# Delta-rule layer: the squares of a head's output placed behind the Xd copy of the next head's solve

## The chip, the cores and the metric

The kernel runs on one core of one Trainium2 chip. The metric is the device time of one execution in microseconds. A core has five engines that work side by side, each through its own queue in order: TensorE (PE; its weight loads are shown apart as PEld), VectorE (DVE), ScalarE (ACT), GpSimd (POOL) and SyncE (SP, which issues most transfers). An engine that waits for a semaphore holds back all that stands behind it in its queue.

## The reference, cut to what matters

The program is a trunk of two layers, each a token mixer and a squared-ReLU MLP, on 512 tokens of 1024 channels. The change lies in the first mixer, a bidirectional gated delta rule with 8 heads of 128 channels:

```python
def _rmsnorm(x, g):
    return x * lax.rsqrt(jnp.mean(x * x, axis=-1, keepdims=True) + RMS_EPS) * g.astype(F32)

def _mixer_gdn(h, w_in, conv_w, a_log, dt_bias, norm_g, w_out):
    ...
    o_f = _gated_delta_chunked(q, k, v, beta[0], g[0])
    o_b = _flip(_gated_delta_chunked(_flip(q), _flip(k), _flip(v), _flip(beta[1]), _flip(g[1])))
    o = (o_f + o_b).transpose(0, 2, 1, 3)
    o = _rmsnorm(o, norm_g) * jax.nn.silu(z.reshape(bn, s, A_HEADS, A_DV))
    return jnp.matmul(o.reshape(bn, s, A_VW).astype(w_out.dtype), w_out)
```

Inside `_gated_delta_chunked` each chunk solves a unit lower triangular system, and a recurrence over the chunks gives the output. The squares of the change are those of `_rmsnorm`: per head, the sums over 128 channels of `o * o` for each of the 512 tokens.

## The kernel before

Products with weights run on PE as three passes: each fp32 operand is split into a high part (a cast on ACT, L96) and a low part (a subtraction on DVE, L101), and `mm3` (L122 to L124) issues high x high, high x low and low x high. These are the *streaming* matmuls of the delta-rule stage: 128x512, 24 for each of the projections to k, q, v and z of a head (tiles pjk, pjq, pjv, pjz), and the output projection (oa).

Each head has four parts. `project` computes k, q, v, z with their short convolutions (DVE, L1405), a Silu on ACT (L1443, with a table load before it and another, L55, behind it) and, in `rows`, the transposes of k and q (tile ktp, L1463), their copy (kt, L1466), their squares (L1468, sums to ssp) and some small exponentials (neg, kds, fq). `solve` inverts the triangular matrices of both directions: it starts from 4x4 blocks, transposes them (xp, L1572), copies them (Xd, L1574), and then doubles the block size in levels of 4, 8, 16, 32 and 64. A level has one product of ath and Dd and two products of Xd and pz (all tile lv, L1600, of 8 matmuls of 128x64 each); a masked copy of the first product to pz stands between (on DVE, but ACT does it at 32, L1614, and a half at 64, L1630). After level 64, ACT copies to Dd (L1635), and a correction product follows (tile nw, L1646). `recur` runs the recurrence (tiles m, vd, vn, sn) and ends with the output product op (L1730), which stays in one PSUM bank of a pool of two. `finish` squares the four 128x128 pieces of op on ACT with an accumulated sum (L1742: junk is thrown away, oss is kept), forms the inverse root (rsy, L196 and L197, and small DVE operations), scales op with it (fo, L1748), transposes (otp, L1752) and multiplies with Silu of z and the norm's weight.

The loop of `gdn` interleaves heads: in round i it issues `recur` of head i-2, `solve` of head i-1, `project` of head i and `finish` of head i-2, in this order; the pairs that the parts yield are not used by `run`. This order of the text is not that of the engines. The framework's scheduler lays out each engine's queue from the dependencies, the order of the text and its own costs, and so a moved instruction moves others. Heads are counted from 0; "in head h" below means within the solve of head h, where the output of head h-1 is squared.

The steps that are touched are ahead of everything in `finish`, and, in `solve`, the copy to Xd:

```python
            T.transpose(xp[:, u, :], dd[:, u, :], g.idh)
        xd = t8("Xd", 1)
        A.copy(xd, xp)
```

Of the kernel before, what the change touches and what calls it, by code (L numbers as in the profile page):

```python
# [8 lines left out]
F32 = mybir.dt.float32  # L9
# [3 lines left out]
AF = mybir.ActivationFunctionType  # L13
# [4 lines left out]
P = 128  # L18
# [3 lines left out]
NT = S // P  # L22
# [1305 lines left out]
def gdn(c, w_in, conv_w, a_log, dt_bias, norm_g, w_out, ln_g, ln_b, x, w_next):  # L1328
    tc, nc = c.tc, c.nc
    with c.banks(ch=2, pj=3, tp=1, ac=2), tc.tile_pool(name="gdn", bufs=1) as pool:  # L1330
        g = GdnConst(c, pool, w_in, a_log, dt_bias, conv_w, norm_g, x)
        hi = [c.big.tile([P, 2, S], F32R, name=f"oh{t}", tag=f"xt{t}") for t in range(NT)]
        lo = [pool.tile([P, 2, S], F32R, name="ol", tag="ol", bufs=NT) for t in range(NT)]
        heads = [GdnHead(c, pool, g, h, w_in, hi[h // 2][:, h % 2, :], lo[h // 2][:, h % 2, :]) for h in range(A_H)]
        for a, b in zip(heads, heads[1:] + [GdnHead(c, pool, g, A_H, w_in, None, None)]):
            a.next = b
        lhs = lambda k, sl: (hi[k // 2][:, k % 2, sl], lo[k // 2][:, k % 2, sl])
        z = [[None, None] for t in range(NT)]
        early = list(range(6))

        def load_z(hf):
            if hf:
                tl = pool.tile([P, NT, S], F32, name="z", tag="sil", bufs=3)
            else:
                tl = heads[-1].next.kq
                more = [heads[-1].t2(tag, n).rearrange("p n i -> p (n i)") for tag, n in (("kt", 3), ("qd", 4))]
            for t in range(NT):
                z[t][hf] = tl[:, t, :] if hf or t < 2 else more[t - 2]
                c.dma(z[t][hf], x[t * P:(t + 1) * P, 512 * hf:512 * hf + 512])

        def run(*gens):
            for gen in gens:
                for _ in gen:
                    pass

        done = set()
        for i in range(A_H + 2):
            old, mid, new = (heads[j] if 0 <= j < A_H else None for j in (i - 2, i - 1, i))
            if old:
                run(old.recur(done))  # L1360
            if mid:
                run(mid.solve(done))
            if new:
                run(new.project(done))
            if i >= A_H:
                load_z(i - A_H)
                run(c.out_pieces(w_out, early, lhs, z, "pj", (i - A_H,), 1))
            if old:
                run(old.finish(done))
        par = c.load_ln(ln_g, ln_b, lambda j: pool.tile([P, S], F32, name="lnp", tag=("ath", "atl", "a4", "Xd")[j]))  # L1370
        c.new_x()
        c.new_xt()
        c.out_last(w_out, [[6, 7]] * 2, lhs, z, ("pj", "ac"), par,
                   [(pool, "oah", "oal", 1), (pool, "ol", "ol", NT)], ahead=lambda: c.take_ahead(w_next, 3))


class GdnHead:
# [8 lines left out]
    def t8(self, name, bufs):  # L1386
        return self.pool.tile([P, 2 * NT, P], F16, name=name, tag=name, bufs=bufs)
# [121 lines left out]
    def solve(self, done):  # L1509

        c, pool, g, h = self.c, self.pool, self.g, self.h
        V, A, T = c.nc.vector, c.nc.scalar, c.nc.tensor
# [59 lines left out]
            T.transpose(xp[:, u, :], dd[:, u, :], g.idh)  # L1572
        xd = t8("Xd", 1)
        A.copy(xd, xp)  # L1574

        def half(t, s, i):

# [95 lines left out]
    def recur(self, done):  # L1673


        c, pool, g, h = self.c, self.pool, self.g, self.h
        V, A, T = c.nc.vector, c.nc.scalar, c.nc.tensor
        ps = self.bank("ktp", tag="tp")
        for n in range(NT):
            T.transpose(ps[:, n, :], self.v[:, n * P:(n + 1) * P], c.ident)  # L1680
        self.vt = self.t2("vt", 2)
        A.copy(self.vt, ps)
        yield 0.0, 1.0
        states, vns = [{}, {}], [{}, {}]
        cur = [None, None]
        for step in range(NT):
            ns = (step, NT - 1 - step)
            rhs = [self.vt[:, n, :] for n in ns]

            def both(name, ops):  # L1690

                ps = self.bank(name, shape=(P, 2, P), tag="ch")
                for d in range(2):
                    T.matmul(ps[:, d, :], *ops(d), start=True, stop=True)  # L1694
                return ps

            if step:
                m1 = both("m1", lambda d: (self.kc(ns[d]), cur[d]))
                for d, n in enumerate(ns):
                    rhs[d] = pool.tile([P, P], F32, name="r", tag="r", bufs=3)  # L1700
                    V.scalar_tensor_tensor(rhs[d], m1[:, d, :], self.pos[:, n, d:d + 1], self.vt[:, n, :], ALU.mult, ALU.subtract)
                yield 0.45, 0.6
            vds = [None, None]
            m2 = both("m2", lambda d: (self.xf[:, d * NT + ns[d], :], rhs[d]))
            for d, n in enumerate(ns):
                states[d][n] = cur[d]
                if step < NT - 1:
                    vds[d] = pool.tile([P, P], F32, name="vd", tag="vd", bufs=3)
                    A.mul(vds[d], m2[:, d, :], self.kds[:, n, d:d + 1])
            for d, n in enumerate(ns):  # L1710
                vn = pool.tile([P, P], F32, name="vn", tag="vn", bufs=9)
                A.mul(vn, m2[:, d, :], -1.0 if step else 1.0)
                vns[d][n] = vn
            yield 0.45, 1.0
            if step < NT - 1:
                m3 = both("m3", lambda d: (self.kt[:, ns[d], :], vds[d]))
                for d, n in enumerate(ns):
                    sn = pool.tile([P, P], F32, name="sn", tag="sn", bufs=10)
                    if cur[d] is None:
                        A.copy(sn, m3[:, d, :])  # L1720
                    else:
                        V.scalar_tensor_tensor(sn, cur[d], g.egl[:, n, d, h:h + 1], m3[:, d, :], ALU.mult, ALU.subtract)
                    cur[d] = sn
                yield 0.45, 0.6
        self.op = op = self.bank("op", tag="ch")
        for n in (1, 2, 0, 3):
            mm = [(self.qke[d][:, n, :], vns[d][n]) for d in range(2)]
            mm += [(self.qd[d][:, n, :], states[d][n]) for d in range(2) if states[d][n] is not None]
            for i, (l, r) in enumerate(mm):
                T.matmul(op[:, n, :], l, r, start=i == 0, stop=i == len(mm) - 1)  # L1730
            if n == 2:
                yield 1.8, 0.0
        done.add(("op", h))

    def finish(self, done):

        c, pool, g, op = self.c, self.pool, self.g, self.op
        V, A, T = c.nc.vector, c.nc.scalar, c.nc.tensor
        ss = c.small.tile([P, NT], F32, name="oss", tag="ss")
        junk = pool.tile([P, P], F32, name="junk", tag="junk", bufs=2)  # L1740
        for n in range(NT):
            A.activation(junk, op[:, n, :], AF.Square, accum_out=ss[:, n:n + 1])  # L1742
        rs_ = c.small.tile([P, NT], F32, name="ors", tag="rs")
        V.tensor_tensor(ss, ss, self.fq2, ALU.mult)
        c.rsqrt(rs_, ss, NT, RMS_EPS, self.fq)
        on = self.t2("fo", 1)
        for n in range(NT):
            A.mul(on[:, n, :], op[:, n, :], rs_[:, n:n + 1])  # L1748
        yield 1.6, 6.0
        otp = self.bank("otp", tag="ch")  # L1750
        for n in range(NT):
            T.transpose(otp[:, n, :], on[:, n, :], c.ident)  # L1752
        p = pool.tile([P, S], F32, name="p", tag="on", bufs=2)
        otp = otp.rearrange("p n i -> p (n i)")
        n = 1 if self.h < A_H - 1 else 2
        for i in range(n):
            sl = slice(i * S // n, (i + 1) * S // n)
            V.scalar_tensor_tensor(p[:, sl], otp[:, sl], g.ng[:, 0:1], self.sz[:, sl], ALU.mult, ALU.mult)
            A.copy(self.ohi[:, sl], p[:, sl])
        for i in range(n):  # L1760
            sl = slice(i * S // n, (i + 1) * S // n)
            V.tensor_tensor(self.olo[:, sl], p[:, sl], self.ohi[:, sl].bitcast(F32), ALU.subtract)
        done.add(("finish", self.h))
        yield 0.45, 0.0
# [39 lines left out]
```

## Time and profile before

| | |
|---|---|
| median of 3 runs | 1340.54 us (1340.32 to 1341.0) |
| the profiled execution, its own time | 1341.23 us |
| its span in the profile | 1339.4 us |
| granted TensorE clock | 0.996 |
| PE busy, first 105 us | 99.79 us |
| PE busy, 400 us to the end (939.40 us) | 924.64 us |
| DMA share, 105 to 400 us / 400 us to the end | 0.20 / 0.53 |

The delta-rule layer takes the first 410 us; the rows between 105 and 400 us, quoted in the prediction, are the rounds in which squares of a head's output stand. How to read the rows: a timeline row has the start in us, the duration in us, the engine, line, operation, tiles as out<-in with their shapes, and the count of merged instructions; in brackets stands the idle time before and what ended it. A row of a table by windows has the stretch, its span, and the busy time and count for PE, PEld, DVE, ACT and POOL, then the granted clock, the DMA share and GB/s. A row of groups has the busy time and mean ns, then the idle time before it and its releasers. An activation with an accumulated sum appears as two records, the ACTIVATE and the reading of its accumulator.

### The profile page before, as it was taken

How to read it: one execution, taken by the hardware profiler on the slowest of the kernel's cores; microseconds unless marked ns; L12 is line 12 of the kernel's file. 1: busy time of each engine (PE TensorE's matmuls, PEld its weight loads, DVE VectorE, ACT ScalarE, POOL GpSimd, SP SyncE). 2: the span in 40 equal slices, each digit the busy share in tenths (PEclk: the TensorE clock that was granted, in tenths of full speed). 3: DMA queues.
4: the chain of work that ended last, by engine and by line, in shares of the span. 5: the costliest groups of instructions: out<-in, count | busy, mean ns of one | idle time of the engine just before them, and what ended most of it. 6: DMA issues, size and time to landing. Idle time of an engine off the chain costs nothing.

```text
span 1339.4 us, 22232 instructions
## 1 busy us (share of the span) xinstructions
PE 1317.2 (98%) x8629; PEld 1124.4 (84%) x8629; DVE 1099.9 (82%) x1802; ACT 800.5 (60%) x1590; POOL 123.3 (9%) x177
## 2 busy tenths in 40 slices
PE   8999999999999999999999999999999999999996
PEld 8777878777777889999998888888889899999985
DVE  6797878788778878988988877967879678989888
ACT  4667657767643645666566754654456456565656
POOL 4000000000000910100102100000001001101011
PEclk9999999999999999999999999999999999999998
DMA  6221112112232674775748532221327475757556
GB/s 179 64 65 47 35 46 64 48 49 72 72 96 63 210 161 149 161 179 150 171 124 176 138 111 71 63 64 63 94 64 208 107 186 137 165 170 147 156 136 148
DMA packets 155660, 154.35 MB, mean 115 GB/s; under 512 B 7723, under 2 KB 122531, under 8 KB 155555
## 3 DMA queue, kind: packets, MB, share of 16 engines
q1 hardware_dynamic: 143779, 110.85, 27.8%
q0 software_dynamic: 11776, 42.08, 16.1%
q8 instruction: 68, 1.11, 0.3%
q14 instruction: 37, 0.30, 0.1%
HBM read 113.99 MB, written 2.10 MB: 87 GB/s over the span
## 4 chain that ended last, share of the span: by engine, by line
PE 86%; DVE 6%; ACT 6%; issue 1%; DMA 1%; DVEq 0%; POOL 0%; ACTq 0%; POOLq 0%
PE pX L123 3%; PE pX L122 3%; PE pX L124 3%; PE fx L124 3%; PE fx L123 3%; PE fx L122 3%; PE pjv L123 3%; PE m L1694 3%; PE pjv L122 3%; PE pjv L124 3%; PE pj L123 3%; PE pj L124 3%; PE pj L122 3%; PE fyz L124 2%; PE fyz L122 2%; PE fyz L123 2%
## 5 line engine op out<-in xcount | busy, mean ns | idle before, releaser
L101 DVE TENSOR_TENSOR wl<-wst,wh 128x1024 fp32r<-128x1024 f32 x148 | 182.3, 1232 | 49.1 <-ACT wh L96 47.8
L96 ACT CAST wh<-wst 128x1024 fp32r<-128x1024 f32 x150 | 157.7, 1051 | 101.1 <-PE fyz L123 30.1
L101 DVE TENSOR_TENSOR w2l<-w2r,w2h 128x1024 fp32r<-128x1024 f32 x92 | 112.7, 1225 | 27.2 <-ACT w2h L96 27.1
L96 ACT CAST w2h<-w2r 128x1024 fp32r<-128x1024 f32 x94 | 98.4, 1048 | 56.3 <-PE pX L124 24.8
L402 POOL DMA_DIRECT2D w2r<-w2r x56 | 48.4, 891 | 503.1 <-DVE w2l L101 290.1
L96 ACT CAST ah<-h 128x1024 fp32r<-128x1024 f32 x56 | 58.8, 1051 | 51.8 <-PE pZ L123 23.2
L451 DVE TENSOR_TENSOR wst<-wst 128x512 f32<-128x512 f32 x110 | 73.5, 688 | 0.2
L101 DVE TENSOR_TENSOR al<-h,ah 128x1024 fp32r<-128x1024 f32 x56 | 68.6, 1224 | 5.2 <-ACT ah L96 5.2
L123 PE MATMUL pX<-w2l,ah 128*128 128x512 f32 x168 | 66.1, 394 | 0.0
L122 PE MATMUL pX<-w2h,ah 128*128 128x512 f32 x168 | 66.0, 393 | 0.0
L124 PE MATMUL pX<-w2h,al 128*128 128x512 f32 x168 | 65.7, 391 | 0.0
L123 PE MATMUL pj<-xtl,wh 128*128 128x256 f32 (+1 forms) x192 | 64.6, 338 | 0.6 <-DVE xtl L188 0.6
L122 PE MATMUL pj<-xth,wh 128*128 128x256 f32 (+1 forms) x192 | 64.2, 338 | 0.3 <-ACT xth L187 0.2
L124 PE MATMUL pj<-xth,wl 128*128 128x256 f32 (+1 forms) x192 | 64.5, 337 | 0.0
L122 PE MATMUL pjv<-wh,xth 128*128 128x512 f32 x128 | 54.4, 425 | 0.0
L124 PE MATMUL pjv<-wh,xtl 128*128 128x512 f32 x128 | 50.2, 392 | 0.0
L123 PE MATMUL pjv<-wl,xth 128*128 128x512 f32 x128 | 50.0, 390 | 0.0
L124 PE MATMUL fx<-xh,wl 128*128 128x256 f32 x176 | 49.7, 283 | 0.0
L124 PE MATMUL fyz<-xh,wl 128*128 128x256 f32 x176 | 49.7, 282 | 0.0
L124 PE MATMUL fx<-xth,wl 128*128 128x256 f32 x176 | 49.7, 282 | 0.0
L123 PE MATMUL fx<-xtl,wh 128*128 128x256 f32 x176 | 49.7, 282 | 0.0
L122 PE MATMUL fyz<-xh,wh 128*128 128x256 f32 x176 | 49.7, 282 | 0.0
(528 smaller groups left out, 4319.1 us busy)
## 6 DMA issues: line engine op xcount, KB each, us to landing
wst<-in_mlp_w SPq DMA_DIRECT2D x68, 512.0 KB, 4.9
w2r<-in_mlp_w SPq DMA_DIRECT2D x60, 512.0 KB, 4.4
w2r<-w2r POOLq DMA_DIRECT2D x56, 512.0 KB, 5.6
wst<-in_a_w_in SPq DMA_DIRECT2D x32, 512.0 KB, 4.0
wst<-in_b_w_in SPq DMA_DIRECT2D x32, 256.0 KB, 3.0
wst<-in_a_w_out SPq DMA_DIRECT2D x8, 512.0 KB, 3.6
wst<-in_b_w_in SPq DMA_DIRECT2D x8, 512.0 KB, 4.2
wst<-in_b_w_out SPq DMA_DIRECT2D x8, 512.0 KB, 3.7
```

Source lines behind the costliest of these rows:

```text
L96: h = nc.scalar.copy(hi, src)
L101: self.halves = h, nc.vector.tensor_tensor(lo, src, hi.bitcast(F32), ALU.subtract)
L122: mm(ps, ah, bh, start=start, stop=False, **kw)
L123: mm(ps, ah, bl, start=False, stop=False, **kw)
L124: self.last_mm = mm(ps, al, bh, start=False, stop=stop, **kw)
L402: nc.gpsimd.dma_start(blocks[a + (q,)], blocks[b + (q,)], accum_op=ALU.add)
L451: plus = lambda a, b: V.tensor_tensor(a, a, b, ALU.add)
L1694: T.matmul(ps[:, d, :], *ops(d), start=True, stop=True)
```

## The change

`finish` loses its squares; a new method `squares` has them, with a tile tag of their own for the sums. `solve` calls it for the head before right behind its Xd copy, so that in the order of the text the squares of head h-1 come ahead of the rest of the solve of head h and of `project` of head h+1. The last head has no solve after it, and its squares stay in `finish`.

```diff
         for a, b in zip(heads, heads[1:] + [GdnHead(c, pool, g, A_H, w_in, None, None)]):
-            a.next = b
+            a.next, b.prev = b, a
+        heads[0].prev = None
...
         xd = t8("Xd", 1)
         A.copy(xd, xp)
+        if self.prev:
+            self.prev.squares()
...
+        self.oss = None
         done.add(("op", h))
+
+    def squares(self):
+
+        c, op = self.c, self.op
+        self.oss = ss = c.small.tile([P, NT], F32, name="oss", tag="oss")
+        junk = self.pool.tile([P, P], F32, name="junk", tag="junk", bufs=2)
+        for n in range(NT):
+            c.nc.scalar.activation(junk, op[:, n, :], AF.Square, accum_out=ss[:, n:n + 1])
 
     def finish(self, done):
 
         c, pool, g, op = self.c, self.pool, self.g, self.op
         V, A, T = c.nc.vector, c.nc.scalar, c.nc.tensor
-        ss = c.small.tile([P, NT], F32, name="oss", tag="ss")
-        junk = pool.tile([P, P], F32, name="junk", tag="junk", bufs=2)
-        for n in range(NT):
-            A.activation(junk, op[:, n, :], AF.Square, accum_out=ss[:, n:n + 1])
+        if self.oss is None:
+            self.squares()
+        ss = self.oss
```

The instructions of every engine are the same in kind and number; their order is not. In the changed kernel a line has a number that is higher by 1 (from the loop in `gdn` on), by 3 (from behind the Xd copy) or by 11 (in `finish`). ACT in head 3, from the Xd copy on, before:

```order
L1574 COPY Xd<-xp 128x1024
L96 CAST wh<-wst 128x1024
L1401 ACTIVATE sil<-pjq,cw 128x512
L96 CAST wh<-wst 128x1024
L1614 CAST pz_135<-lv 32x4x32 x4
L1443 ACT_TABLE_LOAD
L1443 ACTIVATE sil<-sil 128x2048
L1630 ACTIVATE pz_137<-lv 64x4x64
L55 ACT_TABLE_LOAD
L1635 CAST Dd<-lv 64x4x64 x2
```

and now:

```order
L1745 ACTIVATE junk,oss<-op 128x128 x2
L1575 COPY Xd<-xp 128x1024
L1745 ACTIVATE junk,oss<-op 128x128 x2
L96 CAST wh<-wst 128x1024
L1402 ACTIVATE sil<-pjq,cw 128x512
L196 ACTIVATE rsy<-oss,bias_77 128x4
L197 ACTIVATE rsy<-rsy 128x4
L1617 CAST pz_135<-lv 32x4x32 x4
L1633 ACTIVATE pz_137<-lv 64x4x64
L1444 ACT_TABLE_LOAD
L1444 ACTIVATE sil<-sil 128x2048
L1638 CAST Dd<-lv 64x4x64 x2
```

Two squares stand ahead of the Xd copy and two behind it; the first table load and the Silu have moved behind the last pz copy, the other table load behind the Dd copies, and one cast of a weight is gone from here.

ACT in head 5, from the pz copies of level 32 to the Dd copies, before:

```order
L1614 CAST pz_135<-lv 32x4x32 x4
L1468 ACTIVATE junk,ssp<-ktp 128x128
L1742 ACTIVATE junk,oss<-op 128x128
L1468 ACTIVATE junk,ssp<-ktp 128x128
L1742 ACTIVATE junk,oss<-op 128x128
L1468 ACTIVATE junk,ssp<-ktp 128x128
L1742 ACTIVATE junk,oss<-op 128x128
L96 CAST wh<-wst 128x1024
L1630 ACTIVATE pz_137<-lv 64x4x64
```

and now:

```order
L1617 CAST pz_135<-lv 32x4x32 x4
L96 CAST wh<-wst 128x1024
L1402 ACTIVATE sil<-pjv,cw 128x512
L1444 ACT_TABLE_LOAD
L1444 ACTIVATE sil<-sil 128x2048
L1633 ACTIVATE pz_137<-lv 64x4x64
L55 ACT_TABLE_LOAD
L1467 COPY kt<-ktp 128x512
L1638 CAST Dd<-lv 64x4x64 x2
```

The squares are gone, those of k and q come after the Dd copies, and the Silu with its two table loads and the copy of the transposed k stand here instead.

PE in head 5, from the last level product to the correction product nw, before:

```order
L1600 MATMUL lv<-Xd,pz_137 128x64
L122 MATMUL pjz<-xth,wh 128x512
L123 MATMUL pjz<-xtl,wh 128x512
L1646 LDWEIGHTS ath
L1646 MATMUL nw<-Dd,ath 128x128
```

and now:

```order
L1603 MATMUL lv<-Xd,pz_137 128x64
L124 MATMUL pjz<-xth,wl 128x512
L122 MATMUL pjz<-xth,wh 128x512
L123 MATMUL pjz<-xtl,wh 128x512
L124 MATMUL pjz<-xth,wl 128x512
L1649 LDWEIGHTS ath
L1649 MATMUL nw<-Dd,ath 128x128
```

Four streaming matmuls stand between the two products instead of two. The order of PE differs from the solve of head 1 on and is the same again behind the last head's transposes (otp).

## The prediction

> **What bounds the kernel now.** I read the page's busy shares and its chain first, then a table of the delta-rule stage alone, then the timelines of TensorE (PE) and ScalarE (ACT) around the places that the new order changes.
>
> ```profile
> span 1339.4 us, 22232 instructions
> PE 1317.2 (98%) x8629; PEld 1124.4 (84%) x8629; DVE 1099.9 (82%) x1802; ACT 800.5 (60%) x1590; POOL 123.3 (9%) x177
> PE 86%; DVE 6%; ACT 6%; issue 1%; DMA 1%; DVEq 0%; POOL 0%; ACTq 0%; POOLq 0%
> 105.00:400.00 295.00, 292.74 (x2571) 232.89 (x2571) 236.19 (x501) 191.16 (x554) 2.37 (x4) 1.00 0.20 58
> L1742 ACT ACTIVATE junk<-op 128x128 f32<-128x128 f32 x28 | 8.1, 289 | 2.8 <-PE op L1730 2.7
> ```
>
> PE sets the end: busy 98% of the span, 86% of the chain. The fourth row is the stage with the squares (from 105 to 400 us: span, then PE, PEld, DVE, ACT and POOL busy, granted clock 1.00): PE 292.74 of 295.00. ACT works 191.16 of these 295 us, so it has room on average; the 28 squares that the last row counts cost it 8.1 us there and are not what the time is made of. The change leaves the work of every engine as it is. It can only move the short waits of PE, and the page's idle understates them, since a matmul's end is modelled. They are read from start to start:
>
> ```profile
> 120.05 0.50 PE L123 MATMUL pjk<-xtl,wh 128*128 128x512 f32 x1
> 120.68 0.22 PE L1646 MATMUL nw<-Dd,ath 128*128 128x128 f16 x1
> ...
> 293.34 0.48 PE L122 MATMUL pjz<-xth,wh 128*128 128x512 f32 x1
> 293.65 0.40 PE L123 MATMUL pjz<-xtl,wh 128*128 128x512 f32 x1
> 294.41 0.22 PE L1646 MATMUL nw<-Dd,ath 128*128 128x128 f16 x1 [0.36 <-ACT Dd L1635]
> ...
> 380.49 0.40 PE L122 MATMUL oa<-wh,oh 128*128 128x512 f32 x1
> 380.95 0.22 PE L1646 MATMUL nw<-Dd,ath 128*128 128x128 f16 x1
> ...
> 199.24 0.39 PE L123 MATMUL pjz<-xtl,wh 128*128 128x512 f32 x1
> 199.62 0.28 PE L1600 MATMUL lv<-pz,Xd 128*128 128x64 f16 x4
> 200.17 0.28 PE L1600 MATMUL lv<-pz,Xd 128*128 128x64 f16 x4 [0.27 <-ACT pz L1614]
> ...
> 331.38 0.39 PE L124 MATMUL pjz<-xth,wl 128*128 128x512 f32 x1
> 331.99 0.33 PE L1463 MATMUL ktp<-ident,sil 128*128 128x128 f32 x1 [0.22 <-ACT junk L1468]
> ```
>
> A streaming 128x512 matmul lets the next one start 0.23 us later (0.31 when it is the first after short ones: 293.34 to 293.65). Before the correction product nw the step is 0.63 us in head 1, 0.76 in head 5 and 0.46 in head 7: PE waits for ACT's Dd copies. Over heads 1 to 7 (the first and the last of the seven are quoted) the steps exceed 0.23 by 2.2 us, and those of heads 2 to 6, by the same reading, by 1.55. Waits of the same kind stand before the level products (200.17) and the transposes of k (331.99).
>
> **The change part by part.** *What moves.* Four squares per head leave their places between the squares of k and q and go behind (or, where the output is there early, in front of) the Xd copy of the next solve. The order shows that for heads 0 to 5; the squares of head 6 keep their places, one ahead of Xd and three behind, and those of head 7 stay in `finish`. No DMA moves past another but one weight load ahead of two loads of x at the very end of the stage, which I cost at nothing: these loads have the whole output projection before their first use. No table load is added: the count of ACT instructions is the same. I go through the places where the new order makes PE wait or spares a wait.
>
> *Xd held by two squares (heads 2, 3 and 5).* The xp transposes run right behind the output product, and Xd now queues behind two squares.
>
> ```profile
> 188.39 0.39 PE L1730 MATMUL op<-sn,qd 128*128 128x128 f32 x2
> 189.06 0.40 PE L1600 MATMUL lv<-Dd,ath 128*128 128x64 f16 x8
> 189.30 0.48 PE L122 MATMUL pjq<-xth,wh 128*128 128x512 f32 x1
> 190.33 0.41 PE L1600 MATMUL lv<-pz,Xd 128*128 128x64 f16 x8
> ...
> 189.26 1.01 ACT L1574 COPY Xd<-xp 128x1024 f16<-128x1024 f16 x1 [3.13 <-PE xp L1572]
> ...
> 364.92 0.39 PE L1730 MATMUL op<-sn,qd 128*128 128x128 f32 x2
> 365.34 0.28 ACT L1742 ACTIVATE junk<-op 128x128 f32<-128x128 f32 x1 [2.68 <-PE op L1730]
> 365.62 1.01 ACT L1574 COPY Xd<-xp 128x1024 f16<-128x1024 f16 x1
> 366.53 0.28 ACT L1742 ACTIVATE junk<-op 128x128 f32<-128x128 f32 x1
> 366.94 0.28 ACT L1742 ACTIVATE junk<-op 128x128 f32<-128x128 f32 x1
> ```
>
> Head 7 has the new pattern already, with one square: it starts 0.42 after the last pair of op starts (364.92 to 365.34), Xd 0.28 behind it; two squares stand 0.41 apart. In head 3 that gives 188.39 + 0.42 + 0.41 + 0.28 = 189.50 for Xd, against 189.26. There the product with Xd starts 190.33, just as Xd ends (190.27), four streaming matmuls behind the product before it, so the 0.24 reaches PE; head 5 has the same cover, head 2 seven matmuls, which hide it. **+0.48 us**, bounded by 0 (the squares end with xp) and 1.4 (0.69 in both).
>
> *Squares of k and q alone.*
>
> ```profile
> 330.77 0.30 ACT L1742 ACTIVATE junk<-op 128x128 f32<-128x128 f32 x1
> 331.02 0.30 ACT L1468 ACTIVATE junk<-ktp 128x128 f32<-128x128 f32 x1
> 331.27 0.32 ACT L1742 ACTIVATE junk<-op 128x128 f32<-128x128 f32 x1
> ...
> 335.17 0.28 ACT L1468 ACTIVATE junk<-ktp 128x128 f32<-128x128 f32 x1
> 335.57 0.28 ACT L1468 ACTIVATE junk<-ktp 128x128 f32<-128x128 f32 x1
> ```
>
> Alternating squares start 0.25 us apart, squares into one accumulator 0.40. Taking one of a pair away thus saves 0.10, not 0.25. In head 2 three stand alone before the last pz copy, which makes it 0.3 later, and three small exponentials now come ahead of the Dd copies, some 0.2 more: **+0.5** (0 to 0.75).
>
> *Table loads between the last pz copy and the Dd copies.* With the squares gone the scheduler finds other gaps for the loads around Silu.
>
> ```profile
> 203.38 0.38 ACT L1630 ACTIVATE pz<-lv 64x256 f16<-64x256 f32 x1
> 203.77 1.28 ACT L55 ACT_TABLE_LOAD   x1
> 205.07 0.76 ACT L1635 CAST Dd<-lv 64x256 f16<-64x256 f32 x2
> 205.73 0.58 ACT L1466 COPY kt<-ktp 128x512 f32<-128x512 f32 x1
> ...
> 201.43 1.92 ACT L1443 ACTIVATE sil<-sil 128x2048 f32<-128x2048 f32 x1
> ...
> 341.57 1.06 ACT L1443 ACTIVATE sil<-sil 128x1024 f32<-128x1024 f32 x1
> ```
>
> The Dd copies need the last two level products; a product takes PE 0.24 (189.06 to 189.30). Head 5: load 1.28, kt 0.48 (0.58 less the 0.10 that it overlaps its neighbour, 205.07 + 0.76 to 205.73) and Dd 0.76 make 2.52 us behind pz; PE has the two products (0.48) and four streaming matmuls (0.31 + 3 x 0.23) there, 1.48, so nw waits about **1.0**. Head 3: load, Silu and Dd make 3.96; PE has three streaming matmuls, the products, eleven streaming ones and two short ones, 4.1, of which 0.45 have passed when pz ends: **0.3**. Head 6, with the short Silu (1.06) and three small exponentials (0.4), has 3.5 against 5 + 8 streaming matmuls and the products, 3.6, of which 0.7 have passed: **0.6**. Sum +1.9; 0 if Dd's own input is the later, 3.0 if the loads also wait for their input.
>
> [...]
>
> *More changes of stream.* Counted in the order, streaming and short matmuls change over 521 times in the stage instead of 517; at 0.08 (0.31 less 0.23): **+0.3**.
>
> *Gains.* In front of nw heads 2 to 6 now have 3, 11, 3, 4 and 8 streaming matmuls instead of 2, 3, 2, 2 and 4. Each hides 0.23, so the 1.55 us of waits there go (what replaces them is charged above): **-1.55** (0 to -2.2). Of the waits at the level products, head 3's cast of a weight ahead of the pz copies is gone, head 4 has seven matmuls of cover instead of three, and in head 6 the k transposes stand elsewhere: I take -0.35, -0.5 and -0.5, with -0.2 for head 5: **-1.55** (0 to -3).
>
> *Sum.* 0.48 + 0.5 + 1.9 + 0.3 - 1.55 - 1.55 = +0.1 us. The profiled execution took 1341.23 us (span 1339.4), 0.69 over the median 1340.54 of the three runs, so the forecast on the median is **1340.6 us**.
>
> **The rivals.** *Faster by the covers.* The scheduler lengthened the covers where PE waited; if the input of Dd is later than ACT in heads 3, 5 and 6, the 1.9 and the 0.5 fall away: 1340.54 + 0.8 - 3.1 = 1338.2, and with all bounds of the gains 1336.1; I write 1337. For it: the longer covers at five of seven places. Against: the loads stand in ACT's order ahead of Dd, and ACT runs in order. Chance 0.16.
>
> *Slower through ACT's chain.* One mechanism: behind Xd, ACT's way to the Dd copies gets longer in every solve, because the squares stand alone (0.15 more for each of four squares of k and q, 0.6 a head) and the table loads have come in between. It decides from the point where the step before nw exceeds the 0.76 of today's worst. Six heads at about 0.45 beyond my 3.2, with the gain at nw alone: 3.2 + 2.7 - 1.55 = +4.4, 1344.9 us. For it: ACT already releases most of PE's waits here. Against: PE's order gives it more matmuls to wait with. Chance 0.15. [...]
>
> **How the numbers follow.** A measurement of this kernel tells about 0.2%, 2.7 us, from no change. The forecast, gains and losses that cancel within that, has 0.66; faster 0.16, slower 0.15 and 0.02, and 0.01 for what I have not seen. With every term at its lower bound the sum is -4.9, with every term at its upper +5.5; half way from the forecast that is 1338.1 to 1343.3, and I reach 0.6 further on both sides, into the two rivals: range 1337.4 to 1343.8. Faster 0.15, same 0.67, slower 0.18.
>
> **What would show it.** Xd in heads 3 and 5 starts about 1.1 us behind the last pair of op, and the product with Xd about 0.24 later than now. The step before nw is 0.23 to 0.31 in heads 2 and 4, over 0.5 in heads 3, 5 and 6. PE's busy time between 105 and 400 us stays within 1 us. [...]

## The result and the profile after

| | before | changed |
|---|---|---|
| median of 20 runs each | 1340.1 us | 1342.55 us |
| ratio, 95% interval | | 1.0018 [1.0012, 1.0025] |
| the profiled execution, its own time | 1341.23 us | 1342.4 us |
| its span, granted clock | 1339.4 us, 0.996 | 1340.7 us, 0.997 |

The changed kernel takes 2.45 us more than the kernel before. That is inside the range and below the 0.2% that the prediction set as the bound, and yet the interval lies wholly above 1: a small loss, which 20 runs of each can tell from none. One of the 20 runs of the changed kernel took 1608.05 us at a granted clock of 0.849, and the ratio leaves it out. The page of the changed kernel (span; busy time, share and count by engine; the chain by engine):

```profile
span 1340.7 us, 22227 instructions
PE 1317.6 (98%) x8629; PEld 1122.6 (84%) x8629; DVE 1100.4 (82%) x1802; ACT 801.9 (60%) x1590; POOL 123.3 (9%) x177
PE 86%; DVE 6%; ACT 5%; DMA 1%; issue 1%; SPq 0%; DVEq 0%; ACTq 0%
```

Its table by windows (stretch, its length, busy time and count of PE, PEld, DVE, ACT and POOL, granted clock, DMA share, GB/s):

```profile
105.00:400.00 295.00, 292.88 (x2563) 232.47 (x2562) 236.71 (x502) 192.52 (x554) 2.37 (x4) 1.00 0.20 58
```

In the stage that the change reorders PE's busy time is 292.88 us, 0.14 more than before. Such a window cuts both kernels at the same clock time, not at the same work. I therefore cut at PE's instructions. Four of them stand in the same place of PE's order in both kernels: the first transpose of xp in head 1, the last otp of the delta-rule layer, the first projection pj of the first MLP, and the last matmul of the program. First before, then the changed kernel, each from PE's timeline:

```profile
104.96 0.51 PE L1572 MATMUL xp<-idh,Dd 128*128 128x128 f16 x6
...
410.04 0.27 PE L1752 MATMUL otp<-ident,fo 128*128 128x128 f32 x1
...
425.39 0.40 PE L122 MATMUL pj<-xth,wh 128*128 128x256 f32 x2
...
1327.71 0.39 PE L124 MATMUL pX<-xh,al 128*128 128x512 f32 x1
```

```profile
103.98 0.51 PE L1573 MATMUL xp<-idh,Dd 128*128 128x128 f16 x6
...
409.15 0.27 PE L1763 MATMUL otp<-ident,fo 128*128 128x128 f32 x1
...
424.49 0.40 PE L122 MATMUL pj<-xth,wh 128*128 128x256 f32 x2
...
1328.96 0.39 PE L124 MATMUL pX<-xh,al 128*128 128x512 f32 x1
```

From xp to otp, the stage that holds every reordered instruction: 305.08 us before, 305.17 now. From otp to pj: 15.35 and 15.34. From pj to the last matmul: 902.32 before, **904.47** now. (These two executions also differ by 0.98 us ahead of xp; that moves from execution to execution: pj starts at 425.39 and 424.49 here, at 423.22 and 423.40 in the next two kernels.) The loss lies behind the stage, where PE runs the same instructions in the same order. No single step between two matmuls there has grown by more than 0.013 us. The 2.15 us are spread over 5251 steps, 0.4 ns each on average, and no wait stands out. The tile view (durations min/median/max in ns, then first and last start) shows it on one product of the MLPs, before and then changed:

```profile
L122 PE MATMUL fyz<-xh,wh x176: 277/282/388, 505.2 to 1282.6; 128*128 128x256 f32 x176
```

```profile
L122 PE MATMUL fyz<-xh,wh x176: 279/284/387, 504.5 to 1283.7; 128*128 128x256 f32 x176
```

The median is 2 ns longer, the minimum too.

What reaches that far is the one part of the diff that the prediction did not cost: the name of the tile for the sums. The sums had shared the name "ss"; now they have a name of their own, with four buffers of 32 bytes in each partition. In the built programs all tiles of the layers' pools therefore lie 128 bytes higher (h of the first MLP at byte 95104 instead of 94976 of a partition), while the split weights (wh, wl) and the split input of the projections (xth, xtl), which lie ahead of them, stay where they were.

### The profile page after: what moved, and what is told of

It reads as the page before. It is cut to its first block, busy times and chain, and to the rows that moved or that the text cites. A ratio compares the mean times of both kernels' runs of the same rounds, so it can differ in the third digit from the quotient of the medians.

```text
span 1340.7 us, 22227 instructions
## 1 busy us (share of the span) xinstructions
PE 1317.6 (98%) x8629; PEld 1122.6 (84%) x8629; DVE 1100.4 (82%) x1802; ACT 801.9 (60%) x1590; POOL 123.3 (9%) x177
## 4 chain that ended last, share of the span: by engine, by line
PE 86%; DVE 6%; ACT 5%; DMA 1%; issue 1%; SPq 0%; DVEq 0%; ACTq 0%
PE pX L122 3%; PE pX L124 3%; PE pX L123 3%; PE fx L124 3%; PE fx L123 3%; PE fx L122 3%; PE pjv L123 3%; PE pjv L122 3%; PE pjv L124 3%; PE m L1697 3%; PE pj L123 3%; PE pj L124 3%; PE pj L122 3%; PE fyz L122 2%; PE fyz L123 2%; PE fyz L124 2%
## 5 line engine op out<-in xcount | busy, mean ns | idle before, releaser
L123 PE MATMUL fx<-xl,wh 128*128 128x256 f32 x176 | 49.8, 283 | 0.0
L123 PE MATMUL fyz<-xl,wh 128*128 128x256 f32 x176 | 49.7, 283 | 0.0
L122 PE MATMUL fx<-xh,wh 128*128 128x256 f32 x176 | 49.7, 282 | 0.0
```

The source lines that it names most:

```text
L122: mm(ps, ah, bh, start=start, stop=False, **kw)
L123: mm(ps, ah, bl, start=False, stop=False, **kw)
```

## The experiments

### Place against order

The first three kernels separate the two: the kernel before with the new name only, the changed order with the old name, and the changed kernel once more.

The new name only:

```diff
-        ss = c.small.tile([P, NT], F32, name="oss", tag="ss")
+        ss = c.small.tile([P, NT], F32, name="oss", tag="oss")
```

> The kernel before with one word changed: the sums of the squares have a tile tag of their own, as in the changed kernel; the order of every engine is that of before. The tag adds four small buffers, so every tile of the layers' pools lies 128 bytes higher in SBUF, as in the changed kernel. Theory L (the slowdown comes from where tiles lie, not from the order): +2 us or more over before, almost all of it behind the delta-rule stage. Rival S (it comes from the order of the squares): within 0.7 us of before. Rival C (drift between executions): within 0.7 us, and the changed kernel on this chip too.

The changed kernel with the old name:

```diff
-        self.oss = ss = c.small.tile([P, NT], F32, name="oss", tag="oss")
+        self.oss = ss = c.small.tile([P, NT], F32, name="oss", tag="ss")
```

> The changed kernel with the sums of the squares put back under the tag that they shared before; its order on every engine is that of the changed kernel, its tiles lie where those of the kernel before lie. Theory L: within 0.7 us of before. Rival S: +2 us or more, as the changed kernel. Rival C: within 0.7 us.

The changed kernel, unchanged:

> The changed kernel once more, on the chip of the two others. Theory L and rival S: +1.6 to +3.3 us over before, as measured (ratio 1.0012 to 1.0025). Rival C: within 0.7 us.

PE's timeline from the first pj to the last matmul, the new name only and then the changed order with the old name:

```profile
423.22 0.40 PE L122 MATMUL pj<-xth,wh 128*128 128x256 f32 x2
...
1327.65 0.39 PE L124 MATMUL pX<-xh,al 128*128 128x512 f32 x1
```

```profile
423.40 0.40 PE L122 MATMUL pj<-xth,wh 128*128 128x256 f32 x2
...
1325.41 0.39 PE L124 MATMUL pX<-xh,al 128*128 128x512 f32 x1
```

904.43 us with the new name alone, 902.01 with the old name and the new order, beside 902.32 before and 904.47 changed. The times say the same, each ratio taken to runs of the kernel before on the same chip (median 1339.4 us there): 1.0018 [1.0009, 1.0027] for the name alone, 1.0004 [0.9995, 1.0013] for the order alone, 1.0018 [1.0010, 1.0027] for both. The name carries the loss. What the order is worth cannot be told from nothing by these times.

### How the place works

If the place in SBUF is the cause, other shifts should move the part behind the stage too, and by a rule. The kernel before, with the new name and another number of buffers (2, 8, 12, 16, and later 1 and 3), shifts the tiles by 32 bytes for each; PE's order does not change.

```diff
-        ss = c.small.tile([P, NT], F32, name="oss", tag="ss")
+        ss = c.small.tile([P, NT], F32, name="oss", tag="oss", bufs=2)
```

> The kernel before, in its own order, with every tile of the layers' pools 64 bytes higher in SBUF (two spare buffers for the sums). Read from the trace: time on TensorE from the first projection matmul of the first MLP to the last matmul, which was 903.2 us before (trace) and some 2 us more with a shift of 128 bytes. Theory P (the cost goes by the address modulo a power of two): anything from 0 to +2 us, the same in every execution. Rival M (more is worse): between 0 and +2 us. Rival A (any other place is as bad): +2 us.

> The same with 256 bytes. Theory P: +0 +- 0.2 us if the period is 256 or less, else another value. Rival M: over +2 us. Rival A: +2 us.

> The same with 384 bytes. Theory P: as with 128 bytes (+2 us) if the period is 256; its own value if it is 512. Rival M: more than with 256. Rival A: +2 us.

> The same with 512 bytes. Theory P: +0 +- 0.2 us if the period is 512 or less. Rival M: the most of all. Rival A: +2 us.

> The kernel before, with the output sums in a tile name of their own and one buffer of it: 32 bytes, so that the layers' tiles lie 32 bytes higher than before. Theory P (the step between consecutive matmuls goes by the operands' addresses, with a period of 256 bytes): the part behind the stage, first step of the first MLP to the last matmul, comes out between that of no shift and that of 64 bytes, 900.6 to 902.3 us, if the step falls off evenly with the address; on the 0 value, 902.2 to 902.3, if only whole blocks of 64 bytes count. Rival A (some chance of the run): anywhere from 900 to 905 and not by a rule. The stage itself stays at 305.1 to 305.4 us in each case.

> The same with three buffers: a shift of 96 bytes, halfway between the 64 that gave 900.60 us and the 128 that gave 904.5 us behind the stage. Theory P: between 900.6 and 904.5 us, near 902.5 if it goes evenly with the address, at 900.6 if only whole blocks of 64 bytes count. Rival A: by no rule. The stage stays at 305.1 to 305.4 us.

Measured, in us, one execution each, by the same cuts (by them the 903.2 us of the first expectation are 902.32); the columns MLP 1 and MLP 2 are the parts from the first pj to the start of the second layer's mixer and from one and the same pj of the second MLP, 29 us behind its first, to the end:

| shift, bytes | stage | pj to the end | MLP 1 | MLP 2 |
|---|---|---|---|---|
| 0 (before) | 305.08 | 902.32 | 327.79 | 294.68 |
| 32 | 304.98 | 901.41 | 328.26 | 293.80 |
| 64 | 305.24 | 900.60 | 327.31 | 293.73 |
| 96 | 305.34 | 902.58 | 327.18 | 295.59 |
| 128 (new name only) | 305.27 | 904.43 | 329.08 | 295.54 |
| 256 | 305.18 | 902.20 | 327.79 | 294.67 |
| 384 | 305.12 | 904.46 | 329.09 | 295.56 |
| 512 | 305.37 | 902.37 | 327.80 | 294.68 |

0, 256 and 512 bytes give the same MLP times to 0.01 us, and so do 128 and 384 to 0.02: over these shifts the effect repeats every 256 bytes. At 64 bytes all three expectations missed: the part came out 1.72 us shorter, where none had it below 0. Whole blocks of 64 are refuted (32 differs from 0, 96 from 64). The sums at 32 and 96 bytes, 901.41 and 902.58, would fit an even slope, but the two MLPs apart do not: at 32 bytes the first is slower than unshifted and the second faster, at 96 the first is the fastest of all and the second among the slowest. Chance of the execution is out, since executions of the same shift agree so closely. The steps from the start of a matmul to the next one's, averaged by me over the first MLP, show where the time lies (ns):

| | 0 | 32 | 64 | 96 | 128 | 256 |
|---|---|---|---|---|---|---|
| fyz<-xh,wh (88, 256 columns) | 119.3 | 119.8 | 117.4 | 117.1 | 122.7 | 119.4 |
| fx<-xh,wh (256 columns) | 117.1 | 118.5 | 116.3 | 117.9 | 120.1 | 117.1 |
| pX<-w2h,al (84, 512 columns) | 231.0 | 226.8 | 231.1 | 229.3 | 232.6 | 231.0 |

Kernels with the same shift agree within 0.3 ns in each cell (fyz at 64 bytes: 117.4, 117.6 and 117.6 in three executions). Each pair of operands has its own curve. That the place of the layers' tiles sets the step is thus shown. It does not go by a matmul's own operands alone: xth, xtl, wh and wl stay in place in all these kernels, and yet the 44 steps of fx<-xth,wh that have only matmuls of these four tiles around them (two ahead, three behind) take 118.7, 120.0, 120.1, 119.4, 118.0 and 118.6 ns at the six shifts. Nor does it need work of DVE or ACT at the same time: the steps of fyz<-xh,wh in which both stand idle take 117.7 ns unshifted and 121.0 with 128 bytes (7 and 8 steps; 117.3 and 120.8 with 256 and 384). What it is that the accesses meet in, and whether transfers have a part, is not shown.

### The hold of Xd by itself

The prediction's best-founded loss was the 0.24 us by which two squares hold Xd in heads 3 and 5. This kernel has the changed order under the old name, with all four squares tied behind the copy:

```diff
-        A.copy(xd, xp)
+        cp = A.copy(xd, xp)
         if self.prev:
-            self.prev.squares()
+            with c.tc.issue_after(cp.ins):
+                self.prev.squares()
```

> The changed kernel with the output sums under the old tile name (no shift) and with all four squares of an output issued behind the Xd copy, also in heads 3 and 5, where two of them had gone ahead of it. Theory H (the hold that the prediction charged, 0.24 us in each of these two heads, sets the end of the chain there): Xd starts about 0.26 us behind the last opening of the pair, the product with Xd about 0.2 us earlier in heads 3 and 5 than with the old name alone, and the stage is 0.3 to 0.5 us shorter than its 305.2 us there. Rival R (the time is given back at the next wait, as TensorE has cover work that is then used up sooner): the two steps are short but the stage stays at 305.1 to 305.4 us. Behind the stage both expect 902.0 to 902.4 us.

Head 3 first in the changed kernel, ACT and then PE, and then in this one:

```profile
186.30 0.28 ACT L1745 ACTIVATE junk<-op 128x128 f32<-128x128 f32 x1 [2.68 <-PE op L1733]
...
186.70 0.28 ACT L1745 ACTIVATE junk<-op 128x128 f32<-128x128 f32 x1
...
186.97 1.00 ACT L1575 COPY Xd<-xp 128x1024 f16<-128x1024 f16 x1
```

```profile
185.88 0.39 PE L1733 MATMUL op<-sn,qd 128*128 128x128 f32 x2
...
186.55 0.40 PE L1603 MATMUL lv<-Dd,ath 128*128 128x64 f16 x8
...
188.03 0.41 PE L1603 MATMUL lv<-pz,Xd 128*128 128x64 f16 x8
```

```profile
186.81 1.01 ACT L1575 COPY Xd<-xp 128x1024 f16<-128x1024 f16 x1 [3.13 <-PE xp L1573]
```

```profile
185.94 0.39 PE L1734 MATMUL op<-sn,qd 128*128 128x128 f32 x2
...
186.61 0.40 PE L1604 MATMUL lv<-Dd,ath 128*128 128x64 f16 x8
...
187.88 0.42 PE L1604 MATMUL lv<-pz,Xd 128*128 128x64 f16 x8
```

Xd starts 1.09 us behind the last pair of op in the changed kernel and 0.87 here, as in the kernel before (the expectation's 0.26 holds from the last of the eight xp transposes, at about 186.55, not from the pair of op). The product with Xd follows its predecessor after 1.48 us in the one and 1.27 in the other. Head 5 has the same two numbers. So the hold is real, and tying the squares gives back 0.21 in each of the two heads. But up to a point in head 6, as far as PE's order is the same, this kernel needs 226.59 us from the mark at xp, and the changed order with the old name 226.70: of 0.42 gained, 0.1 is left. Head 2 took most of it. All four squares now stand there behind Xd, ACT reaches the Silu later, and the table load behind it holds the copies that feed a level product. ACT and PE in head 2 of this kernel:

```profile
152.10 1.28 ACT L55 ACT_TABLE_LOAD   x1
153.40 0.59 ACT L1467 COPY kt<-ktp 128x512 f32<-128x512 f32 x1
```

```profile
155.35 0.40 PE L124 MATMUL pjz<-xth,wl 128*128 128x512 f32 x1
156.14 0.28 PE L1604 MATMUL lv<-pz,Xd 128*128 128x64 f16 x4 [0.39 <-ACT pz L1618]
```

PE stands 0.79 us at this step, against 0.42 with two squares ahead of Xd. Mechanism H holds for the hold, and R for the time.

From there on the scheduler uses up PE's cover in another order, which the edit had not asked for. The whole stretch from xp to the first pj grew from 320.58 to 325.01 us, and the one timed run took 1344.07 us. So the stage as a whole cannot be compared, and the expected gain was missed. Where most of the 4.4 us went is seen in PE's timeline at the end of the stage, and in the table by windows:

```profile
410.01 0.40 PE L124 MATMUL ob<-oah,ol 128*128 128x512 f32 x1
410.92 1.10 PE L1764 MATMUL otp<-ident,fo 128*128 128x128 f32 x4 [0.51 <-ACT fo L1760]
413.04 0.50 PE L122 MATMUL ob<-oah,oh 128*128 128x512 f32 x1 [1.01 <-ACT oh L1771]
...
416.20 0.63 PE L122 MATMUL ob<-ol,oh 128*128 128x512 f32 x1
416.62 0.63 PE L123 MATMUL ob<-ol,oh 128*128 128x512 f32 x1
```

```profile
414.00:417.50 3.50, 3.50 (x11) 2.68 (x10) 2.21 (x4) 0.22 (x1) 0.00 (x0) 0.51 0.00 0
```

With no cover left, PE waits for the last head's scaling and cast (0.51 and 1.01 us), and behind that idle time, from 414.07 to 417.48, eight streaming matmuls follow each other after 0.42 us instead of 0.23, at a granted clock of 0.51 by the table's row, which costs about 1.5 us. That the idle time brings the lower clock is not shown.

### A version that is faster than both

A shift of 64 bytes was the best of the scan. It was timed with both orders; the edits are two buffers of the new name in the kernel before (above) and in the changed one.

```diff
-        self.oss = ss = c.small.tile([P, NT], F32, name="oss", tag="oss")
+        self.oss = ss = c.small.tile([P, NT], F32, name="oss", tag="oss", bufs=2)
```

> The kernel before with the layers' tiles 64 bytes higher, as in the look above, now timed. Theory P: behind the stage 900.6 us again, 1.7 us less than without a shift, so about 1.7 us less than the kernel before: a ratio of 0.9987, its interval under 1. Rival A (the 900.6 us were that one execution's): 902.2 us behind the stage and a ratio of 0.999 to 1.001 with 1 within the interval.

> The changed kernel, with two buffers of the new tile name: the squares in the new order, the layers' tiles 64 bytes higher than before. Theory P (order and place add up): stage 305.1 to 305.4 us, behind it 900.5 to 900.8 us, so some 3.7 us less than the changed kernel and 1.6 us less than the kernel before, a ratio of 0.9988. Rival A: behind the stage over 902 us. If the order of the squares by itself were worth a time of its own, this run and the one of the kernel before with the same shift would differ by more than 0.3 us in the stage.

The kernel before with 64 bytes, PE's timeline and the tile view again:

```profile
423.61 0.40 PE L122 MATMUL pj<-xth,wh 128*128 128x256 f32 x2
...
1324.26 0.39 PE L124 MATMUL pX<-xh,al 128*128 128x512 f32 x1
```

```profile
L122 PE MATMUL fyz<-xh,wh x176: 276/279/384, 503.4 to 1279.0; 128*128 128x256 f32 x176
```

| order | shift | stage | pj to the end | median | ratio to before |
|---|---|---|---|---|---|
| before | 0 | 305.08 | 902.32 | 1340.1 | 1 |
| before | 128 | 305.27 | 904.43 | 1341.73 | 1.0018 [1.0009, 1.0027] |
| before | 64 | 305.06 | 900.65 | 1338.39 | 0.9985 [0.9976, 0.9994] |
| changed | 0 | 305.22 | 902.01 | 1340.41 | 1.0004 [0.9995, 1.0013] |
| changed | 128 | 305.34 | 904.16 | 1342.74 | 1.0018 [1.0010, 1.0027] |
| changed | 64 | 305.57 | 900.35 | 1339.45 | 0.9990 [0.9981, 0.9998] |

Each ratio is to runs of the kernel before on the same chip beside it (median 1339.4 us beside the shifts of 0 and 128, 1340.56 beside 64), so dividing the table's medians does not give it. Both versions with 64 bytes beat the kernel before, by little, and with it the changed one; the old order is the better of the two or the same. Place and order add up as far as these times can tell. The last row's stage, 305.57, misses what was expected (at most 305.4, and within 0.3 of the other order's 305.06), and its 900.35 lies 0.15 below what was expected. Against the same order unshifted (305.22), 0.14 lies at one step, the first otp of the last head; the rest is in steps under 0.05. Over all executions the stage is 305.18 on average with the old order (nine, 304.98 to 305.37) and 305.33 with the new one (four, 305.17 to 305.57, the first profile among them). An order that costs 0.1 to 0.2 us would fit this, and is not settled.

## Why the prediction was right, and where it was not

**The stage.** The sum for the reordered stage was +0.1 us, and the stage grew by 0.09 in the first profile and by some 0.15 over all executions, which their spread does not settle. That it came out so well is partly luck: the terms were off in both directions. I add up, over all steps of PE from xp to the last otp, what goes beyond a mark (0.115 us behind a short matmul, where the median step in the kernel before is 0.03 for lv and 0.11 for m, qk and op; 0.235 behind a streaming one, median 0.23; 0.315 behind a streaming one that follows short ones, median 0.315), sorted by the matmul that comes late:

| late is | before | changed |
|---|---|---|
| nw | 2.12 | 0.86 |
| level products lv | 3.76 | 4.07 |
| m and qk | 2.86 | 4.14 |
| kk | 0.53 | 0.28 |
| all others | 8.00 | 7.86 |
| sum | 17.27 | 17.21 |

In this stretch PE changes 424 times between streaming and short matmuls instead of 420, two of the four with the dearer first step, which adds 0.16: +0.10 in all, against 0.09 measured. So close an agreement is chance, since steps below the marks are not counted and the ep products, of 512 columns, count as short ones; counted as streaming, the sum falls by 0.43, and m and qk grow by 1.04.

- *Xd held by two squares, +0.48.* Right in mechanism and size: 1.27 to 1.48 us, 0.21 in each of heads 3 and 5, and undone when the squares were tied behind the copy.
- *Table loads before the Dd copies, +1.9, and the gain at nw, -1.55.* With the +0.5 of head 2 that made +0.85 at nw in heads 2 to 6; measured there are 0.73 us of late steps instead of 1.55, so -0.82. The rest of the -1.26 lies in heads 1 and 7, for which the sum had no term. The gain is there and the loads cost little. In head 5 the load and kt stand where they were expected, but nw starts only 0.48 us behind the matmul ahead of it, not 1.2, because PE had more to do than I counted. ACT, then PE in head 5 of the changed kernel:

```profile
290.15 0.38 ACT L1633 ACTIVATE pz<-lv 64x256 f16<-64x256 f32 x1
290.55 1.28 ACT L55 ACT_TABLE_LOAD   x1
291.84 0.59 ACT L1467 COPY kt<-ktp 128x512 f32<-128x512 f32 x1
292.45 0.76 ACT L1638 CAST Dd<-lv 64x256 f16<-64x256 f32 x2
```

```profile
290.58 0.28 PE L1603 MATMUL lv<-pz,Xd 128*128 128x64 f16 x4
290.69 0.42 PE L1464 MATMUL ktp<-ident,sil 128*128 128x128 f32 x2
290.87 0.47 PE L124 MATMUL pjz<-xth,wl 128*128 128x512 f32 x1
...
292.78 0.40 PE L124 MATMUL pjz<-xth,wl 128*128 128x512 f32 x1
293.26 0.22 PE L1649 MATMUL nw<-Dd,ath 128*128 128x128 f16 x1
```

  Between the two halves of the first product stand two transposes of k and three streaming matmuls, 0.96 us (290.69 to 291.65), which the working had left out. Head 3 shows the same slip: when its pz ends (197.91 + 0.38), PE has not yet begun the product, so nothing of the 4.1 us of cover has passed. ACT needs 4.02 until its second Dd copy ends, PE has 4.30, and nothing waits:

```profile
197.91 0.38 ACT L1633 ACTIVATE pz<-lv 64x256 f16<-64x256 f32 x1 [1.85 <-PE lv L1603]
...
201.55 0.76 ACT L1638 CAST Dd<-lv 64x256 f16<-64x256 f32 x2
```

```profile
198.50 0.29 PE L1603 MATMUL lv<-pz,Xd 128*128 128x64 f16 x4
...
202.37 0.38 PE L1464 MATMUL ktp<-ident,sil 128*128 128x128 f32 x2
202.59 0.22 PE L1649 MATMUL nw<-Dd,ath 128*128 128x128 f16 x1
```

  The prediction's sign, a step over 0.5 in heads 3, 5 and 6, thus failed in all three: 0.11 (behind a transpose), 0.48 and 0.32. Head 4 has 0.24, as expected.
- *Head 2, +0.5.* The step before nw is 0.53 now and was 0.46, and the product at level 64 comes 0.1 later: about +0.2. The sign for this head, a step of 0.23 to 0.31, missed too, and did not go with the charge of 0.5.
- *Gain at the level products, -1.55.* It did not come. Without the 0.42 of the Xd hold the level products gained 0.1. Head 3 gave its share (late steps of 0.35 us instead of 0.64), but heads 4 and 6 lost 0.08 and 0.19 instead of gaining 0.5 each, and head 1, which the sum did not have, lost 0.28.
- *More changes of stream, +0.3.* Undersized, since not only their number counts but what stands beside what. The late steps at m and qk grew by 1.28. The largest of them stand where no input is late by the profile, but where a short matmul, or a single streaming one, now precedes. That cover which now stands ahead of nw is missing there is my reading of it; no run moved it back. In head 5, qk followed a run of streaming matmuls before; now a single one stands between a short matmul and it, and its step is 0.54 instead of 0.23. Before, then changed:

```profile
296.58 0.39 PE L123 MATMUL pjk<-xtl,wh 128*128 128x512 f32 x1
296.81 0.61 PE L1653 MATMUL qk<-sil 128*128 128x128 f32 x4
```

```profile
294.19 0.48 PE L122 MATMUL pjk<-xth,wh 128*128 128x512 f32 x1
294.73 0.71 PE L1656 MATMUL qk<-sil 128*128 128x128 f32 x4
```

**The step that failed** is the one that says "The change leaves the work of every engine as it is" and lets the change move only the short waits of PE. It took everything behind the stage for unchanged and costed the new tile name at nothing. That part cost 2.15 of the 2.45 us, and no wait of the stage has to do with it. That the total still fell into the range is luck: the range was made for gains and losses within the stage, and happened to be wide enough for a term that it did not have. In the unshifted place the forecast for the order, +0.1 us, is not contradicted: the ratio 1.0004 with its interval is -0.7 to +1.7 us.

**The rivals.** *Faster by the covers* was right about nw, where most of the waits went, and wrong that this reaches the end: the late steps at m and qk grew by about as much. *Slower through ACT's chain* fell: the largest step before nw is 0.53, below the 0.76 from which it would decide. The loss has its sign, but another cause. The further 0.02 on the slower side stood for a pause of ACT behind each table load, and no run shows that term: behind the load at 290.55, which takes 1.28, the next ACT instruction starts at 291.84, 0.01 us behind its end. The traces of both kernels have 27 loads of 1.28 us each, and the next instruction of ACT starts 0.01 us behind 25 of them before and 24 in the changed kernel; behind the others it waits for its input and starts 0.02 us after that is there.

## What to carry to other kernels

A diff that gives a tile another name or number of buffers can move all that is allocated behind it in SBUF, and here that was worth from -1.7 to +2.15 us, more than the reordering it came with. Before a small difference is credited to an order, hold the addresses fixed (keep the old name, or pad to the same place), and compare the parts of the program whose order has not changed step by step. And the waits that go at one place can come back at another (late steps here: 1.26 us fewer at nw, 1.28 more at m and qk): add up the late steps of the whole stage, not only where the wait has gone.

## What was not expected of the hardware

- The step between back-to-back matmuls of the MLPs depends on where the layers' tiles lie in SBUF, with a period of 256 bytes over the shifts of 0 to 512: for fyz<-xh,wh with 256 columns 117.1 to 122.7 ns, for pX<-w2h,al with 512 columns 226.8 to 232.6 ns, repeated to 0.3 ns between executions. Matmuls whose own operands stay in place change too, by up to 2.1 ns (fx<-xth,wh, 118.0 to 120.1).
- Some 2.8 us in which PE did only four transposes (410.24 to 413.04), at the end of the stage in the kernel with the tied squares, were followed, four matmuls later, by 3.4 us (414.07 to 417.48) with streaming matmuls 0.42 us apart, at a granted clock of 0.51 (row 414.00 to 417.50); it was 1.00 from 405 to 414 and from 417.5 to 420. The kernel before shows 0.50 as well, from 11 to 13 us, and the changed kernel 1.00 there, although PE is busy about as long from 8 to 12 us (2.40 and 2.36 us). No run shows what brings it.
